# Head-wise sums of squares by four 64x64 products in the quarters of the array

## The chip, the cores and the metric

The kernel runs on one core of one Trainium2 chip. The metric is the device time of one execution in microseconds, from the first to the last instruction and what lies around them; lower is better. The matrix engine is TensorE (PE in the profile, PEld for its weight loads), the others are VectorE (DVE), ScalarE (ACT) and GpSimd (POOL); SyncE (SP) issues most DMAs. The kernel was run three times before the change, with a median of 848.72 us (846.47 to 850.33).

## The reference, cut to what matters

The program computes one layer of a hybrid model on 16 + 512 = 528 tokens of 1024 channels. One input projection of the normalised tokens feeds two groups of eight heads with 64 channels each: RWKV-7 (a recurrence over chunks) and FoX (attention with forgetting). Gates merge them, and an output projection and an MLP follow. What the change touches is a sum of squares over the 64 channels of each head, per token, in three places: RWKV's keys, FoX's queries and FoX's keys.

```python
kk = hv(k * k_k)
kk = kk / jnp.maximum(jnp.sqrt(jnp.sum(kk * kk, axis=-1, keepdims=True)), 1e-12)
...
def head_rmsnorm(t, g):
    tf = t.astype(jnp.float32)
    return tf * lax.rsqrt(jnp.mean(tf * tf, axis=-1, keepdims=True) + NORM_EPS) * g
...
q = head_rmsnorm(q.reshape(Bn, Ln, H_FX, HEAD_DIM), q_gain)
k = head_rmsnorm(k.reshape(Bn, Ln, H_FX, HEAD_DIM), k_gain)
```

## The kernel before

Channels lie on the 128 partitions and tokens along the free dimension, so a tile of 128 partitions holds two heads ("a pair"): head 0 on partitions 0 to 63, head 1 on 64 to 127. There are four pairs in each group. The stage that matters here runs from about 20 to 418 us. Its bulk are 40 blocks of the input projection: each is 128 output channels, made of 8 input blocks times three passes in the type float32r (high times high, high times low, low times high), in two parts of 264 tokens, or in one part of 512 for FoX's queries and for the 16 gate blocks. Their weights arrive as `wraw`, are split by ScalarE into `whi` and by VectorE into `wlo` (L470, L471), and the products go to the PSUM tiles `pj` (L501). Beside them run the recurrent heads (`recurrent`, `chain`, `group_norm`), the FoX features (`fox_features`: sums, normalisation, transposed values) and the attention (`attention`: scores `psc` at L611, transposed weights `ppt` at L640, mixing `py` at L656).

The order on TensorE is written out by a planner while the program is built. Each of these activities is a generator that yields the time from which it can go on, `Turns.run` picks by rank the first that is due on a model clock (`Clock`), and the projections, which have the last rank, fill the rest. In that clock a float32 matmul of the full array costs its columns divided by 600 us, one of a smaller tile columns divided by 1200, and a change of tile shape 0.1 us. TensorE keeps exactly this order; for the other engines a scheduler orders the instructions.

PSUM tiles called "sm" (`psm`, four banks) hold the small products in turn, and `banks(n)` tells when n of them come free.

A sum over the channels of a head is a matmul with `ones_blk`, the 128x128 matrix that is one where row and column belong to the same head and zero elsewhere: out of the squares (`sq`, 128 partitions) it puts each head's sum on all 64 partitions of that head. There are twelve such sums.

- RWKV's keys, one in each of four pairs (`Pair.keys`): two products of 264 columns (L754), each followed by a maximum on VectorE from PSUM into `sq` (L755); then ScalarE's logarithm and exponential (L757, L758) make the inverse root, and VectorE scales the keys `okk` (L761). From them follow `L` (L778, L781), `KT` and `BK` (L766, L767) and, on GpSimd, `BK` and `KT` again (L768 to L772), which the scores `psr` (L807) and the transposes `pbt` (L814) read.
- FoX's queries, one in each of four pairs (`normed`): one product of 512 columns (L553), ScalarE's logarithm straight from PSUM (L555), exponential (L557), and VectorE's scaling (L558).
- FoX's keys, one in each of four pairs: the same in two products of 264 columns.

The scores `psr` at L807 already use the array in quarters: `hss` are the two halves of the partitions, and each product reads one half of the rows and writes one half of the PSUM partitions, in all four combinations.

## Time and profile before

| | us |
|---|---|
| three runs: median (lowest to highest) | 848.72 (846.47 to 850.33) |
| the profiled execution: its own time | 849.18 |
| its span, first to last instruction | 847.4 |
| TensorE busy in the span | 825.8 (97%) |
| VectorE busy | 616.5 (73%) |
| ScalarE busy | 454.2 (54%) |
| GpSimd busy | 135.1 (16%) |

The granted TensorE clock was 0.999 of full speed. In the profile's rows a number such as L553 is a line of the kernel before; a tile name stands without its buffer number; "128*128" after MATMUL is the part of the array in use (rows by columns), and what follows is the shape of the result. Busy times of TensorE are made of modelled ends, so where the cost of a short group is asked, the starts of the matmuls before and behind it say more than the lengths.

### The profile page before, as it was taken

How to read it: one execution, taken by the hardware profiler on the slowest of the kernel's cores; microseconds unless marked ns; L12 is line 12 of the kernel's file. 1: busy time of each engine (PE TensorE's matmuls, PEld its weight loads, DVE VectorE, ACT ScalarE, POOL GpSimd, SP SyncE). 2: the span in 40 equal slices, each digit the busy share in tenths (PEclk: the TensorE clock that was granted, in tenths of full speed). 3: DMA queues.
4: the chain of work that ended last, by engine and by line, in shares of the span. 5: the costliest groups of instructions: out<-in, count | busy, mean ns of one | idle time of the engine just before them, and what ended most of it. 6: DMA issues, size and time to landing. Idle time of an engine off the chain costs nothing.

```text
span 847.4 us, 15278 instructions
## 1 busy us (share of the span) xinstructions
PE 825.8 (97%) x5740; PEld 678.1 (80%) x5740; DVE 616.5 (73%) x1222; ACT 454.2 (54%) x923; POOL 135.1 (16%) x133
## 2 busy tenths in 40 slices
PE   7889999999999999999999999999999999999998
PEld 6878987878887787677788779888888888888886
DVE  6996996679867965665457564876777677768688
ACT  7767536765656337644555452665355435544452
POOL 1041300004012000000022001203700560055000
PEclk9999999999999999999999999999999999999999
DMA  6231231110222212123486422651743274245421
GB/s 229 58 103 58 72 113 43 45 59 26 77 88 87 75 52 89 51 75 113 138 272 218 154 88 82 201 153 51 248 149 100 85 244 132 86 136 189 119 92 74
DMA packets 51338, 95.88 MB, mean 113 GB/s; under 512 B 5816, under 2 KB 6968, under 8 KB 51264
## 3 DMA queue, kind: packets, MB, share of 16 engines
q1 hardware_dynamic: 47680, 86.52, 32.1%
q0 software_dynamic: 1280, 4.20, 1.6%
q10 hardware_dynamic: 2304, 4.20, 1.5%
q8 instruction: 45, 0.74, 0.4%
q14 instruction: 29, 0.24, 0.1%
HBM read 88.57 MB, written 6.31 MB: 112 GB/s over the span
## 4 chain that ended last, share of the span: by engine, by line
PE 80%; DVE 5%; DMA 4%; ACT 4%; issue 2%; POOL 1%; SPq 0%; ACTq 0%; DVEq 0%; POOLq 0%
PE pj L501 25%; PE po L1150 21%; PE po L1268 12%; PE pd L1268 5%; DMA gl<-gd 2%; PE pw L858 2%; PE po L1120 2%; PE psc L611 1%; DMA wraw<-in_wo 1%; PE py L656 1%; PE ppt L640 1%; PE psr L807 1%; PE pssq L553 1%; PE pch L918 1%; PE pch L924 1%
## 5 line engine op out<-in xcount | busy, mean ns | idle before, releaser
L501 PE MATMUL pj<-uhi,whi 128*128 128x264 f32 (+1 forms) x480 | 165.7, 345 | 0.0
L501 PE MATMUL pj<-ulo,whi 128*128 128x264 f32 (+1 forms) x480 | 154.2, 321 | 1.6 <-DVE ulo L401 1.6
L501 PE MATMUL pj<-uhi,wlo 128*128 128x264 f32 (+1 forms) x480 | 154.0, 321 | 0.0
L501 PEld LDWEIGHTS pj<-uhi,whi 128*128 128x128 f32 x480 | 90.2, 188 | 15.0 <-issue 6.7
L501 PEld LDWEIGHTS pj<-ulo,whi 128*128 128x128 f32 x480 | 90.5, 188 | 8.6 <-DVE ulo L401 2.0
L501 PEld LDWEIGHTS pj<-uhi,wlo 128*128 128x128 f32 x480 | 90.3, 188 | 6.9
L236 DVE TENSOR_TENSOR wlo<-wraw,whi 128x512 fp32r<-128x512 f32 x88 | 68.2, 785 | 37.9 <-ACT whi L235 35.6
L1150 PE MATMUL po<-zhi,whi 128*128 128x512 f32 (+1 forms) x248 | 94.8, 382 | 0.0
L1150 PE MATMUL po<-zlo,whi 128*128 128x512 f32 (+1 forms) x248 | 94.8, 382 | 0.0
L1150 PE MATMUL po<-zhi,wlo 128*128 128x512 f32 (+1 forms) x248 | 94.8, 382 | 0.0
L235 ACT CAST whi<-wraw 128x512 fp32r<-128x512 f32 x88 | 53.7, 616 | 51.5 <-DMA wraw<-in_wup 19.3
L471 DVE TENSOR_TENSOR wlo<-wraw,whi 128x512 fp32r<-128x512 f32 x80 | 61.9, 781 | 17.5 <-ACT whi L470 17.0
L470 ACT CAST whi<-wraw 128x512 fp32r<-128x512 f32 x80 | 49.1, 618 | 43.8 <-PE pj L501 43.2
L270 ACT CAST whi<-t 128x512 fp32r<-128x512 f32 x64 | 39.9, 623 | 44.4 <-DVE wlo L271 20.6
L271 DVE TENSOR_TENSOR wlo<-t,whi 128x512 fp32r<-128x512 f32 x64 | 49.4, 784 | 18.8 <-ACT whi L270 18.0
L1268 PE MATMUL po<-wlo,fhi 128*128 128x512 f32 x160 | 62.7, 392 | 0.2 <-DVE wlo L271 0.2
L1268 PE MATMUL po<-whi,flo 128*128 128x512 f32 x160 | 62.3, 390 | 0.0
L1268 PE MATMUL po<-whi,fhi 128*128 128x512 f32 x160 | 62.0, 389 | 0.0
L1196 POOL TENSOR_TENSOR t<-traw 128x512 f32<-128x512 f32 x24 | 35.3, 1475 | 154.0 <-DVE wlo L271 135.8
L1150 PEld LDWEIGHTS po<-zhi,wlo 128*128 128x128 f32 x248 | 46.6, 188 | 9.0
L1150 PEld LDWEIGHTS po<-zhi,whi 128*128 128x128 f32 x248 | 46.6, 188 | 9.0
L1150 PEld LDWEIGHTS po<-zlo,whi 128*128 128x128 f32 x248 | 46.6, 188 | 9.0
(307 smaller groups left out, 1758.5 us busy)
## 6 DMA issues: line engine op xcount, KB each, us to landing
wraw<-in_win SPq DMA_DIRECT2D x84, 256.0 KB, 2.6
wraw<-in_wup SPq DMA_DIRECT2D x64, 256.0 KB, 3.4
wraw<-in_wdn SPq DMA_DIRECT2D x48, 256.0 KB, 2.6
traw<-in_wdn SPq DMA_DIRECT2D x48, 256.0 KB, 3.1
gd<-gt ACTq DMA_DIRECT2D x16, 256.0 KB, 2.3
wraw<-in_wout SPq DMA_DIRECT2D x16, 256.0 KB, 2.9
gl<-gd SPq DMA_DIRECT2D x16, 256.0 KB, 3.5
wraw<-in_wo SPq DMA_DIRECT2D x16, 256.0 KB, 3.3
```

Source lines behind the costliest of these rows:

```text
L235: A.copy(hi, raw)
L236: low.tensor_tensor(lo, raw, hi.bitcast(F32), ALU.subtract)
L270: A.copy(hi, x)
L271: V.tensor_tensor(lo, x, hi.bitcast(F32), ALU.subtract)
L470: A.copy(hi, raw)
L471: low.tensor_tensor(lo, raw, hi.bitcast(F32), ALU.subtract)
L501: mm(po, a, b[:, k, a0:a1], start=n == 0, stop=n == 23)
L858: mm(ps_[hs, n - b0, :], lhs(n)[hs], rhs(n)[hs], start=True, stop=True)
L1120: mm(po, a[:, k, 128 * i:128 * i + 128], b[:, k, :], start=n == 0, stop=n == 23)
L1150: mm(po[:, t0:t1], a, b[:, k, t0:t1], start=n == 0, stop=n == 23)
L1196: eng.tensor_tensor(t, sums[c, pair] if c in (T1, T2) else c, d, ALU.add)
L1268: mm(x[i], a[:, k, left, 128 * i:128 * i + 128], c, start=start and k == 0 and n == 0, stop=stop and k == n_pairs - 1 and n == 2)
```

## The change

Each sum is made of four products of 64 rows, 64 columns of the array and half of the tokens, in place of one or two products with the full array. The first half of the tokens goes from each half of the partitions to the same half in PSUM; the second half goes across, head 0 to partitions 64 to 127 and head 1 to 0 to 63, into a second PSUM tile. So the four products stand in the four quarters. The first PSUM tile is read by one instruction of 128 partitions as before, the second by two of 64 that put each head back in its place. Queries, which had one product and one evacuation, now have two tiles and three evacuations and ask for two free banks. The request for the activation table (`pinned`) comes behind all products.

```diff
--- before.py
+++ after.py
@@ -546,14 +546,19 @@
                 def normed(d, parts, gcol):
                     yield d["in"]
                     f, sq = d["f"], d["sq"]
-                    yield lambda: max(ck.ready(sq), banks(len(parts)))
+                    yield lambda: max(ck.ready(sq), banks(2))
                     pin = None
-                    for a0, a1 in parts:
-                        pq = psm("pssq")[:, :a1 - a0]
-                        mm(pq, ones_blk, sq[:, a0:a1], start=True, stop=True)
-                        pin = pin or pinned(d["s"])
-                        after(act(sq[:, a0:a1], pq, AF.Ln, bias=eps, scale=1.0 / 64), pin)
                     c0 = parts[0][0]
+                    half = (T - c0) // 2
+                    cuts = [slice(c0, c0 + half), slice(c0 + half, T)]
+                    pqs = [psm("pssq")[:, :half] for i in range(2)]
+                    for turn, (pq, cols) in zip((1, -1), zip(pqs, cuts)):
+                        for hs, os in zip(hss, hss[::turn]):
+                            mm(pq[os], ones_blk[hs, hs], sq[hs, cols], start=True, stop=True)
+                    pin = pinned(d["s"])
+                    for turn, (pq, cols) in zip((1, -1), zip(pqs, cuts)):
+                        for hs, os in ((slice(0, 128),) * 2,) if turn > 0 else zip(hss, hss[::-1]):
+                            after(act(sq[hs, cols], pq[os], AF.Ln, bias=eps[hs], scale=1.0 / 64), pin)
                     act(sq[:, c0:], sq[:, c0:], AF.Exp, scale=-0.5)
                     V.scalar_tensor_tensor(f, f, gcol, sq[:, c0:], ALU.mult, ALU.mult)
                     return f
@@ -749,10 +754,14 @@
                 self.sq = sq = rp.tile([128, TP], F32, name="sq")
                 s_ = act(sq[:, :T], okr, AF.Square, scale=self.col(C_KK))
                 yield lambda: max(ck.ready(sq), banks(2))
-                for hc in (slice(0, HT), slice(HT, T)):
-                    pq = psm("pkk")[:, :HT]
-                    mm(pq, ones_blk, sq[:, hc], start=True, stop=True)
-                    V.tensor_scalar(sq[:, hc], pq, 1e-24, None, ALU.max)
+                cuts = [slice(0, HT), slice(HT, T)]
+                pqs = [psm("pkk")[:, :HT] for i in range(2)]
+                for turn, (pq, hc) in zip((1, -1), zip(pqs, cuts)):
+                    for hs, os in zip(hss, hss[::turn]):
+                        mm(pq[os], ones_blk[hs, hs], sq[hs, hc], start=True, stop=True)
+                for turn, (pq, hc) in zip((1, -1), zip(pqs, cuts)):
+                    for hs, os in ((slice(0, 128),) * 2,) if turn > 0 else zip(hss, hss[::-1]):
+                        V.tensor_scalar(sq[hs, hc], pq[os], 1e-24, None, ALU.max)
                 pin = pinned(s_)
                 after(act(sq[:, :T], sq[:, :T], AF.Ln), pin)
                 act(sq[:, :T], sq[:, :T], AF.Exp, scale=-0.5)
```

The planner's clock sees other costs, so the order moves. Three places follow, before the change and with it; later lines of the changed program have higher numbers (L807 is L816, L814 is L823).

TensorE, the sum for FoX's keys of the second head pair (`pssq`), inside the chain of states (`pch`, `pyy`, transposed values `pvt`). Before:

```order
L924 MATMUL pch<-Rs,Tt 64x64 x4
L904 MATMUL pvt<-cs,ov 64x128 x2
L553 MATMUL pssq<-fsq,cs 128x264 x2
L939 MATMUL pch<-uv,bkT 64x64 x4
L947 MATMUL pyy<-uv,L_705 64x64
```

With the change:

```order
L927 MATMUL pch<-uv,L_1117 64x64
L557 MATMUL pssq<-fsq,cs 64x264 x4
L933 MATMUL pch<-Rs,Tt 64x64 x4
L913 MATMUL pvt<-cs,ov 64x128 x2
L643 MATMUL ppm<-cs,pe 16x128
```

Two products are four, and the sum has moved from behind the transposes to ahead of the state product with Tt, which uses quarters as well.

VectorE, the keys of the first head pair, from the key factor (`sg`) to KT. Before:

```order
L760 TENSOR_TENSOR sg<-sg,okk 128x528
L471 TENSOR_TENSOR wlo<-wraw,whi 128x512
L755 TENSOR_SCALAR sq<-pkk 128x264 x2
L314 MEMSET tm 128x1
L318 SCALAR_TENSOR_TENSOR orr<-pj,pr_65,tm 128x264
L471 TENSOR_TENSOR wlo<-wraw,whi 128x512
L761 SCALAR_TENSOR_TENSOR okk<-okk,pr,sq 128x528
L778 SCALAR_TENSOR_TENSOR L_705<-okk,P 128x9x63
```

With the change:

```order
L769 TENSOR_TENSOR sg<-sg,okk 128x528
L471 TENSOR_TENSOR wlo<-wraw,whi 128x512
L764 TENSOR_SCALAR sq<-pkk 128x264
L764 TENSOR_SCALAR sq<-pkk 64x264 x2
L314 MEMSET tm 128x1
L318 SCALAR_TENSOR_TENSOR orr<-pj,pr_65,tm 128x264
L471 TENSOR_TENSOR wlo<-wraw,whi 128x512
L770 SCALAR_TENSOR_TENSOR okk<-okk,pr,sq 128x528
L471 TENSOR_TENSOR wlo<-wraw,whi 128x512
L787 SCALAR_TENSOR_TENSOR L_708<-okk,P 128x9x63
```

There is one maximum more, and a conversion of weights that stood behind the second L now stands ahead of the first.

ScalarE, the logarithms for FoX's keys of the first head pair, with the evacuation of the values (`vf`). Before:

```order
L793 ACTIVATE bv<-bv,pr 128x512
L555 ACTIVATE fsq<-pssq,eps 128x264 x2
L557 ACTIVATE fsq<-fsq 128x528
L567 COPY vf<-pj 128x264
L470 CAST whi<-wraw 128x512 x2
```

With the change:

```order
L802 ACTIVATE bv<-bv,pr 128x512
L572 COPY vf<-pj 128x264
L561 ACTIVATE fsq<-pssq,eps 128x264
L561 ACTIVATE fsq<-pssq,eps 64x264 x2
L562 ACTIVATE fsq<-fsq 128x528
L470 CAST whi<-wraw 128x512 x2
```

Two logarithms are three, and a copy of the values has moved ahead of them.

## The prediction

> **What bounds the kernel now.** I read the page's first part and the chain that ended last first, then the windows by stage, then TensorE's own waits, and last the timeline around single sums. One matmul of the source in plain float32 stands in these views as two records, so the two 264-column products of one sum are "x4".
>
> ```profile
> PE 825.8 (97%) x5740; PEld 678.1 (80%) x5740; DVE 616.5 (73%) x1222; ACT 454.2 (54%) x923; POOL 135.1 (16%) x133
> PE 80%; DVE 5%; DMA 4%; ACT 4%; issue 2%; POOL 1%; SPq 0%; ACTq 0%; DVEq 0%; POOLq 0%
> ```
>
> TensorE is busy for 97% of the span and makes 80% of the chain. The sums that change lie between 46 and 319 us, inside the stretch in which projections fill every hole in TensorE's queue. Its windows (busy us and instruction count per engine, granted clock, DMA share, GB/s):
>
> ```profile
> 20.00:72.00 52.00, 46.92 (x391) 40.41 (x390) 47.62 (x90) 34.82 (x67) 9.99 (x12) 1.00 0.24 72
> 72.00:120.00 48.00, 48.00 (x381) 43.46 (x380) 39.89 (x83) 26.92 (x52) 10.23 (x10) 1.00 0.24 74
> 140.00:200.00 60.00, 58.02 (x612) 45.20 (x610) 41.91 (x137) 44.72 (x123) 3.15 (x4) 1.00 0.15 46
> 200.00:260.00 60.00, 60.00 (x507) 52.65 (x505) 46.69 (x113) 36.61 (x80) 8.86 (x10) 1.00 0.23 72
> 340.00:417.00 77.00, 76.92 (x578) 55.46 (x575) 43.78 (x141) 38.23 (x101) 0.00 (x0) 1.00 0.26 83
> ```
>
> The first column after the length is TensorE: full from 72 to 120 and from 200 to 260 us, 2 us short between 140 and 200, and full again to the end of the stage at 417. So a microsecond less of TensorE work brings the end of the stage forward by nearly one. Only the first window is different: there 5 us are idle and VectorE has 47.6 of 52 us. TensorE's waits on other engines between 40 and 345 us, ten in all, the longest and the shortest:
>
> ```profile
> PE ppt L638 <- DVE pe L627: 1.3, 1, 1.3
> PE pkk L754 <- ACT sq L750: 0.7, 1, 0.7
> PE pbt L814 <- DVE L L810: 0.4, 1, 0.4
> ```
>
> None is longer than 1.3 us and none waits for what follows a sum directly.
>
> **What the twelve sums cost now.** The groups by line and shape:
>
> ```profile
> L754 PE MATMUL pkk<-sq,cs 128*128 128x264 f32 x16 | 4.4, 399 | 0.7 <-ACT sq L750 0.7
> L553 PE MATMUL pssq<-fsq,cs 128*128 128x264 f32 x16 | 4.2, 386 | 0.0
> L553 PE MATMUL pssq<-fsq,cs 128*128 128x512 f32 x8 | 4.1, 592 | 0.0
> ```
>
> Sixteen records are eight products, thus four sums of keys (L754) and four of FoX keys (L553), 528 columns each; the last row is four sums of queries, 512 columns. Records overlap, so I take cost from starts. The timeline around one sum (start, length, engine):
>
> ```profile
> 81.50 0.28 PE L501 MATMUL pj<-uhi,wlo 128*128 128x264 f32 x1
> 81.62 1.05 PE L754 MATMUL pkk<-sq,cs 128*128 128x264 f32 x4
> 82.32 0.48 PE L501 MATMUL pj<-uhi,whi 128*128 128x264 f32 x1
> 82.64 0.28 PE L501 MATMUL pj<-ulo,whi 128*128 128x264 f32 x1
> ```
>
> From 81.50 to 82.64 are 1.14 us; two projection matmuls are in it, each 0.12 (81.50 to 81.62). The sum costs 0.90 us, or 1.70 ns a column. Eight such and four of 512 columns (0.87) make 10.7 us.
>
> **What the new form costs.** Four 64x64 products in the four quarters have a precedent, the score products of L807: twelve products of 128 columns (24 records) as four quarters, three times over. And a switch to another shape, two products of 64 rows side by side, stands at L611:
>
> ```profile
> 91.88 0.28 PE L501 MATMUL pj<-uhi,wlo 128*128 128x264 f32 x1
> 92.09 0.89 PE L807 MATMUL psr<-L,BK 64*64 64x128 f32 x24
> 92.90 0.39 PE L501 MATMUL pj<-uhi,whi 128*128 128x264 f32 x1
> 93.13 0.29 PE L501 MATMUL pj<-ulo,whi 128*128 128x264 f32 x1
> ...
> 280.14 0.39 PE L501 MATMUL pj<-uhi,wlo 128*128 128x512 f32 x1
> 280.46 0.73 PE L611 MATMUL psc<-ka,qa 64*128 64x272 f32 x4
> 281.12 0.50 PE L501 MATMUL pj<-uhi,whi 128*128 128x512 f32 x1
> 281.46 0.40 PE L501 MATMUL pj<-ulo,whi 128*128 128x512 f32 x1
> 281.69 0.39 PE L501 MATMUL pj<-uhi,wlo 128*128 128x512 f32 x1
> ```
>
> 91.88 to 93.13 is 1.25, less two projections 1.01 us. Two at a time would need six rounds of 128 columns, 1.31 us, which is more than all of it; four at a time need 0.65. So all four quarters ran at once, and 0.36 us went into leaving the full array and coming back, 0.18 for each change of shape. At L611: 1.32 less two projections of 0.23 (281.46 to 281.69) is 0.86, and 272 columns two at a time are 0.46, which leaves 0.40, or 0.20 a change. A sum by quarters between two projections is then 0.45 + 0.36 = 0.81 us against 0.90: half of the streaming is saved and nearly all of it paid back in switching.
>
> [...]
>
> Not every sum stands alone. In the order of the changed program eight of twelve lie between full-array matmuls on both sides, four touch a neighbour of another shape, and counted over TensorE's whole order the changes of shape go from 304 to 321: 17 more. So the sum on TensorE: streaming 8 x 0.45 + 4 x 0.435 = 5.3, changes 17 x 0.18 = 3.1, together 8.4 instead of 10.7: **2.3 us less**. The bounds: if changes cost nothing, 5.3 less; if the quarters ran only two at a time (at L807 two products in the same rows read the same columns, here they read different halves, which no row shows), 3.1 more, and with 24 changes of 0.20, 4.8 more. I take 2.3 less, because L807 uses the same shape and data type.
>
> **What is added behind the sums.** The second half comes out with its heads exchanged and needs two instructions of 64 partitions instead of one. The rows of the evacuations, and two copies that show that fewer partitions are not faster:
>
> ```profile
> L555 ACT ACTIVATE fsq<-pssq,eps 128x264 f32<-128x264 f32 x8 | 3.4, 475 | 0.1
> L555 ACT ACTIVATE fsq<-pssq,eps 128x512 f32<-128x512 f32 x4 | 2.8, 688 | 0.6 <-PE pssq L553 0.6
> L755 DVE TENSOR_SCALAR sq<-pkk 128x264 f32<-128x264 f32 x8 | 3.4, 431 | 2.0 <-PE pkk L754 1.9
> L906 ACT COPY uv<-pvt 64x256 f32<-64x256 f32 x36 | 13.1, 364 | 8.8 <-PE pvt L904 8.1
> L541 ACT COPY ka<-pj 128x264 f32<-128x264 f32 x8 | 3.0, 371 | 0.0
> ```
>
> ScalarE: a query sum 3 x 0.47 for 0.69 (+0.72), a FoX key sum 3 x 0.475 for 2 (+0.475), times four 4.8 us. VectorE: 4 x 0.43 = 1.7 us. Both engines have room (36.6 and 46.7 of 60 us between 200 and 260), so this is no load. It is delay: the last evacuation of a key sum ended 0.90 + 0.43 = 1.33 us after the first matmul began and now 0.18 + 0.45 + 3 x 0.43 = 1.92, +0.59; for FoX keys 0.90 + 0.475 = 1.38 becomes 2.05, +0.67; for queries 0.87 + 0.69 = 1.56 becomes 2.02, +0.46. Projections cover it, unless TensorE has none to run while it waits. That is so at one place, the first head pair:
>
> ```profile
> 49.37 0.69 DVE L471 TENSOR_TENSOR wlo<-wraw,whi 128x512 fp32r<-128x512 f32 x1 [0.91 <-ACT whi L470]
> 58.91 1.43 POOL L772 TENSOR_TENSOR KT<-BK,P 64x576 f32<-64x576 f32 x1
> 60.39 0.55 PE L814 MATMUL pbt<-cs,KT 128*128 128x128 f32 x3 [0.49 <-POOL KT L772]
> 61.94 0.87 PE L807 MATMUL psr<-L,BK 64*64 64x128 f32 x20 [0.64 <-DVE Bm L808]
> 63.18 0.52 PE L814 MATMUL pbt<-cs,KT 128*128 128x128 f32 x3 [0.38 <-DVE L L810]
> ```
>
> In the changed order VectorE has one evacuation more (0.43) and a weight conversion (0.69) ahead of the products that make KT, so the wait of the transposes on GpSimd's KT grows from 0.49 by up to 1.1 us. Queued behind them are the scores' second group and its evacuations. Against this, the conversion that moved forward is one less ahead of Bm, and the two waits on VectorE there, 0.64 and 0.38, may go: +0.1 to +1.1, I take **+0.6**. Nothing else waits for a sum: FoX's queries and keys go to scores that come several blocks later.
>
> Net: -2.3 + 0.6 = **-1.7 us**. The profiled execution took 849.18 us (span 847.4 and 1.8 around it), so 847.5. The median of the three runs shown is 0.5 lower, 848.72, which gives 847.0; I state 847.2. A measurement of this kernel tells about 0.5%, 4.2 us, from no change, so this forecast is "no change".
>
> **Rivals.**
> - *Switching hides.* If leaving and returning overlap with the full-array matmuls next to them, 5.3 - 0.6 = 4.7 us are gained: 844.0 to 844.5. Against it: 0.36 and 0.40 in two rows above. 8%.
> - *Two at a time, slower.* If two quarters that share rows cannot stream different columns at once, the streaming stays 10.7 and switching comes on top: +3.1 to +4.8, with the 0.6 852.4 to 854.1. It decides as soon as a sum takes over 0.90 us. For it: L807 never streams different columns in the same rows. Against it: each quarter's product is an instruction with a stream of its own there too. 9%.
> - *The later evacuations reach TensorE, slower.* All of the delay is 4 x 0.59 + 4 x 0.67 + 4 x 0.46 = 6.9 us; if all were waited for, 6.9 - 2.3 = +4.6, 853.3. It decides from a third on, when it eats the 2.3. The order also shifts projections around the chain of states between 140 and 200 us, where waits of 1.3 us exist already. Against it: windows full of TensorE work. 12%.
> - *The gain stops at the stage's end.* If what lies behind 417 us does not start earlier, 848.7. Against it: the first matmul there waits for evacuations that follow the last projection, and shifts with it. 10%.
>
> The forecast keeps 61%, with 845 to 850 as its own range, since a reordered program can win or lose a wait or two of 1.3 us. The range for 8 in 10 goes most of the way to the first and the second rival: **843.0 to 853.0**. Faster by over 0.5% (below 844.5): half of the first rival, a few favourable reorderings, 0.11. Slower (above 853.0): half of the second, a third of the third and a little, 0.11. Within: 0.78.
>
> **What would show it.** In the profile after: a lone sum between projections should take 0.75 to 0.85 us by starts, with its eight records begun nearly together in two groups (right), or 1.2 us and more (two at a time). Evacuations of 64 partitions should cost as much as those of 128. TensorE's wait on KT near 60 us should be 1 to 1.6 us, and the last projection should end one to three microseconds before 417.9. I am wrong if a lone sum takes 0.5 us, or if a new wait of several microseconds stands behind an evacuation.

## The result, and the profile after

The changed kernel takes **851.77 us** in the median of twenty runs (849.36 to 855.80), the kernel before 848.98 us in twenty runs beside them (846.47 to 851.02). The ratio is 1.0035, with a 95% interval of 1.0025 to 1.0045: 0.35% slower. A second group of twelve runs of the same changed program (called `changed_again` below) gave 851.33 us and 1.0015 (1.0002 to 1.0028). The change is inside the range that was forecast and within 0.5% of no change, but it went the other way: 2 to 3 us were lost where 1.7 were to be gained.

The profiled execution of the changed kernel took 855.80 us, which is the longest of its twenty. Where one nearer to the middle is needed I read `changed_again`, whose profiled execution took 852.65 us (span 850.8); it is the longest of its twelve, 1.3 us above their median. The first rows of the page of the one and the other: busy time per engine, and the shares of the chain that ended last, `changed_again` first and the slower execution behind it.

```profile
PE 825.6 (97%) x5796; PEld 675.3 (79%) x5796; DVE 617.6 (73%) x1226; ACT 457.4 (54%) x935; POOL 133.0 (16%) x133
PE 79%; DVE 6%; ACT 5%; DMA 2%; issue 2%; POOL 1%; DVEq 0%; ACTq 0%; POOLq 0%
```
```profile
PE 827.8 (97%) x5796; PEld 676.2 (79%) x5796; DVE 618.3 (72%) x1226; ACT 457.1 (54%) x935; POOL 134.7 (16%) x133
PE 75%; DVE 6%; ACT 5%; DMA 5%; issue 2%; POOL 2%; SPq 0%; DVEq 0%; ACTq 0%; POOLq 0%
```

TensorE has 56 records more (each sum now has eight), yet its busy time did not fall. The sum itself does what was forecast. The timeline of TensorE in the changed kernel, around the sum that was shown of before (start, length, engine):

```profile
81.00 0.28 PE L501 MATMUL pj<-uhi,wlo 128*128 128x264 f32 x1
81.21 0.68 PE L761 MATMUL pkk<-sq,cs 64*64 64x264 f32 x8
81.82 0.39 PE L501 MATMUL pj<-uhi,whi 128*128 128x264 f32 x1
82.05 0.28 PE L501 MATMUL pj<-ulo,whi 128*128 128x264 f32 x1
82.17 0.29 PE L501 MATMUL pj<-uhi,wlo 128*128 128x264 f32 x1
```

From 81.00 to 82.05 are 1.05 us; less two projections of 0.12 the sum costs 0.81 us, against 0.90 before. So the four quarters do run together: at the 1.70 ns a column of the sum before, their four times 264 columns two at a time would take 0.90 us, and four at a time 0.45. As an estimate from that, 0.36 of the 0.45 us that they save goes into the two changes of shape. The evacuations of 64 partitions cost what those of 128 cost: the groups of the changed kernel by line, with the shortest, median and longest in ns.

```profile
L561 ACT ACTIVATE fsq<-pssq,eps x24: 461/474/482, 76.2 to 320.0; 64x256 f32<-64x256 f32 x8, 64x264 f32<-64x264 f32 x8, 128x256 f32<-128x256 f32 x4, 128x264 f32<-128x264 f32 x4
L764 DVE TENSOR_SCALAR sq<-pkk x12: 420/430/435, 47.6 to 264.7; 64x264 f32<-64x264 f32 x8, 128x264 f32<-128x264 f32 x4
```

What is new stands in TensorE's waits between 40 and 345 us (engine, tile, line, what it waited for: us in total, times, longest). Five of the fourteen of `changed_again`:

```profile
PE pw L867 <- DVE AX L861: 2.2, 1, 2.2
PE ppt L643 <- DVE tm L314: 1.1, 1, 1.1
PE psc L616 <- DVE y_rw L995: 0.8, 1, 0.8
PE psc L616 <- DVE L L819: 0.5, 1, 0.5
PE pbt L823 <- POOL KT L781: 0.5, 1, 0.5
```

The wait on KT near 60 us is as short as before. The longest wait, 2.2 us, is that of the second group's inverse (`pw`) on VectorE's `AX`; the kernel before does not wait there at all. The windows show the place: of the kernel before and then of `changed_again` between 260 and 320 us (length, then busy us of TensorE, its weight loads, VectorE, ScalarE, GpSimd, granted clock, DMA share, GB/s).

```profile
260.00:320.00 60.00, 58.54 (x696) 48.49 (x696) 48.92 (x114) 26.32 (x62) 7.03 (x5) 1.00 0.21 67
```
```profile
260.00:320.00 60.00, 57.02 (x625) 45.98 (x624) 48.43 (x117) 26.64 (x64) 6.30 (x5) 0.97 0.22 67
```

Two things are in the second fence that I had not looked for: TensorE is 1.5 us emptier, and the granted clock is 0.97. The clock is not evenly lower: in this profile it is 0.50 from 277.8 us on for 3.41 us and full on both sides. That is 1.7 us of a full clock, as much as the whole gain that was forecast.

**The stage's sum.** For each kernel I cut the projection stage, from the first projection matmul to the last, into four parts: the streaming of all columns, TensorE's waits over 0.05 us, 1.7 us for each stretch at half clock (half of its 3.41 us), and the rest, in which the changes of shape stand. The streaming is worked out from the columns and not measured, so the rest takes up whatever that leaves; only the differences between the kernels count.

| | before | after | changed_again |
|---|---|---|---|
| stage, us | 383.6 | 385.0 | 386.3 |
| streaming | 333.5 | 328.2 | 328.2 |
| changes of shape and rest (changes) | 42.4 (296) | 46.7 (313) | 46.4 (313) |
| waits | 7.7 | 10.05 | 9.9 |
| half clock in the stage | 0 | 0 | 1.7 |
| last projection to last matmul, us | 425.1 | 429.7 | 426.1 |

The streaming falls by 5.2 us: that is half of the 6272 columns of the sums at 600 a us, the rate in the planner's clock; at the 1.70 ns a column that a sum took by starts it would be 5.3. Changes of shape and rest take 4.0 to 4.3 us of it back; what is in them follows in the section on the prediction. The waits take 2.2 us more, so that the stage is 1.0 to 1.4 us longer before any loss of clock. Behind the stage `changed_again` loses another 1.0 us. The slower execution loses 4.6 there: one stretch at half clock (1.7), waits that are 1.7 us longer, and 1.2 that I have not traced.

### The profile page after: what moved, and what is told of

It reads as the page before. It is cut to its first block, busy times and chain, and to the rows that moved or that the text cites. A ratio compares the mean times of both kernels' runs of the same rounds, so it can differ in the third digit from the quotient of the medians.

```text
span 854.0 us, 15403 instructions
## 1 busy us (share of the span) xinstructions
PE 827.8 (97%) x5796; PEld 676.2 (79%) x5796; DVE 618.3 (72%) x1226; ACT 457.1 (54%) x935; POOL 134.7 (16%) x133
## 4 chain that ended last, share of the span: by engine, by line
PE 75%; DVE 6%; ACT 5%; DMA 5%; issue 2%; POOL 2%; SPq 0%; DVEq 0%; ACTq 0%; POOLq 0%
PE pj L501 22%; PE po L1159 20%; PE po L1277 12%; PE pd L1277 5%; PE po L1129 2%; PE pw L867 2%; DMA gl<-gd 1%; DMA wraw<-in_wo 1%; PE py L661 1%; PE psc L616 1%; PE psr L816 1%; PE ppt L645 1%; POOL gl L1084 1%; PE pch L933 1%; DVE wlo L236 1%
## 5 line engine op out<-in xcount | busy, mean ns | idle before, releaser
L236 DVE TENSOR_TENSOR wlo<-wraw,whi 128x512 fp32r<-128x512 f32 x88 | 71.3, 819 | 37.5 <-ACT whi L235 37.5
L471 DVE TENSOR_TENSOR wlo<-wraw,whi 128x512 fp32r<-128x512 f32 x80 | 61.8, 782 | 12.9 <-ACT whi L470 12.6
```

The lines of the kernel that those rows point to most:

```text
L236: low.tensor_tensor(lo, raw, hi.bitcast(F32), ALU.subtract)
L471: low.tensor_tensor(lo, raw, hi.bitcast(F32), ALU.subtract)
```

## The experiments

Each kernel's ratio is to runs of the kernel before on the same chip and in the same hour. Lines of these kernels are a few numbers off those of before and after, since they carry a list. To hold the order fixed, the planner's choices were recorded from one kernel and played back in another: `Turns.run` then takes the listed stream, and a second list gives the PSUM bank of each projection block. The list by itself costs nothing that shows: the kernel before, played back from its own list (`before_warm` of experiment 5, which is changed only behind the stage), has a stage of 383.6 us, as without it.

```diff
-            at = next((i for i, t in enumerate(times) if t + self.ROOM[self.streams[i][0]] <= ck.pe + ck.SLACK), None)
+            now = turns.pop(0)
+            at = next(i for i, s in enumerate(self.streams) if s[1] == now)
```

**1. The change again: how steady is the result?** No edit.

> The changed kernel once more, for a second profile and for times on the same chip as the next three. Both theories: 851 to 853 us, about 1.0035 times before. Theory A (the planner's new order makes the loss) expects again one new wait of about 2 us near 306 us, TensorE's L867 on VectorE's L861; theory B (the quarters and their three evacuations make it) expects the loss to be spread over the twelve sums.

Measured: 851.33 us, 1.0015 (1.0002 to 1.0028). Still slower, though by less than in the first group. The waits in the stage agree with the first profile's to 0.1 us; the stretch at half clock lies elsewhere (277.8 us instead of 502.5). So the waits belong to the program and the place of the half clock does not. Both theories had expected 851 to 853 us.

**2. Is it the order or the new form?** The quarters of the change in the order of the kernel before, and the other way round, sums by the full array in the order of the changed kernel. The two edits are the change and its reverse, each with the list of the other order:

```diff
 q_in_old: the kernel before, its own order listed
-                    mm(pq, ones_blk, sq[:, hc], start=True, stop=True)
-                    V.tensor_scalar(sq[:, hc], pq, 1e-24, None, ALU.max)
+                    for hs, os in zip(hss, hss[::turn]):
+                        mm(pq[os], ones_blk[hs, hs], sq[hs, hc], start=True, stop=True)
...
 full_in_new: the changed kernel, its own order listed
-                    for hs, os in zip(hss, hss[::turn]):
-                        mm(pq[os], ones_blk[hs, hs], sq[hs, hc], start=True, stop=True)
+                    mm(pq, ones_blk, sq[:, hc], start=True, stop=True)
```

> The sums by quarters as in the change, but the planner's choices are taken from the kernel before, written out as a list, so TensorE's order is that of before except for the twelve sums themselves (changes of tile shape 319, before 304, changed 321). Theory A (the new order makes the loss): -5.2 us of streaming, 15 changes of shape at 0.18 are +2.7, up to +1 for later evacuations: ratio to before 0.997 to 0.999, 846.5 to 848.3 us. Theory B (the quarters themselves): still slower, ratio 1.002 to 1.005, 850.7 to 853.2 us.

> The sums with the full array and the evacuations as before, but with the planner's choices of the changed kernel, so TensorE runs in the changed order. Theory A: the order's loss without the quarters' gain, ratio 1.003 to 1.007, 851.5 to 855 us, with the wait near 306 us. Theory B: as before, ratio 0.999 to 1.001.

Measured: quarters in the old order 854.84 us, 1.0060 (1.0041 to 1.0079); full sums in the new order 852.51 us, 1.0036 (1.0022 to 1.0050). Neither theory stands alone. The new order by itself loses about 3 us without any quarter, and the quarters by themselves lose about 5 us in the old order, more than theory B allowed. The two do not add up: together they lost 2 to 2.8 us. In the profile of the full sums in the new order the wait of `pw` is there, and in that of the quarters in the old order the wait near 198 us has grown (the kernel before, then the quarters in its order):

```profile
PE pw L862 <- DVE AX L856: 2.2, 1, 2.2
```
```profile
PE ppt L638 <- DVE pe L627: 1.3, 1, 1.3
```
```profile
PE ppt L647 <- DVE pe L636: 1.8, 1, 1.8
```

**3. Which part of the new form?** Two kernels in the old order, each with a part of the change. `diag_in_old` puts two 64x64 products on the diagonal in place of each full one, with the evacuations as before. `split_in_old` leaves the products full, in halves of the tokens, and takes only the three evacuations.

```diff
 diag_in_old
-                    mm(pq, ones_blk, sq[:, hc], start=True, stop=True)
+                    for hs in hss:
+                        mm(pq[hs], ones_blk[hs, hs], sq[hs, hc], start=True, stop=True)
...
 split_in_old
-                    V.tensor_scalar(sq[:, hc], pq, 1e-24, None, ALU.max)
+                    for hs, os in ((slice(0, 128),) * 2,) if turn > 0 else zip(hss, hss):
+                        V.tensor_scalar(sq[hs, hc], pq[os], 1e-24, None, ALU.max)
```

> The order of before; each full-array product is replaced by two 64x64 products on the diagonal (head 0 to its own half, head 1 to its own), with the evacuations of before. Streaming stays as it was (two side by side), so this prices the changes of shape alone: 15 more than before. Theory A, with 0.18 a change: +2.7 us, ratio 1.003, a lone sum 0.90 + 0.36 = 1.26 us by starts. Theory B, in which a switch costs more than the rows showed, for instance in the weight loads behind it: over +4 us, ratio above 1.005.

> The order of before and full-array products, but each sum in two halves of the columns with the evacuations of the change: both products first, then one instruction of 128 partitions and two of 64. No change of tile shape is added (304). It prices the later evacuations alone: from the waits that stand in the trace of the quarters in the old order, +0.5 to +2 us of waits, and where one of them passes 1.6 us a half-clock stretch more; ratio 1.0005 to 1.004.

Measured: 853.07 us, 1.0043 (1.0027 to 1.0059), and 852.56 us, 1.0035 (1.0020 to 1.0051). Either part alone costs at least as much as the whole change. The first lies between its two theories. It loses on TensorE: nothing is saved in streaming, and the changes of shape and rest add up to 44.7 us (311 changes) against 42.4 (296); its stage is 1.6 us longer, and two windows at half clock behind the stage, 3.4 us, do the rest in its profile. The second has no change of shape more, and TensorE's streaming and rest are those of before within 0.5 us. Its stage is nevertheless 3.9 us longer: waits of 8.6 us against 7.7, and two stretches at half clock, 3.4 us. Without the clock's part most of the second result has no explanation; over all its executions the clock took 2.0 us of the 2.8 (the table behind experiment 7).

**4. When does the clock halve?** In the quarters in the old order it halves twice in the stage. Windows of 3.41 us that end and begin where it changes (columns as above; the granted clock is the third figure from the end):

```profile
193.36:196.77 3.41, 3.37 (x43) 2.59 (x39) 2.63 (x13) 2.45 (x8) 1.17 (x1) 1.00 0.24 79
196.77:200.18 3.41, 1.62 (x21) 1.19 (x23) 3.32 (x9) 1.73 (x5) 0.00 (x0) 1.00 0.00 0
200.18:203.59 3.41, 3.41 (x16) 2.60 (x13) 2.67 (x8) 0.89 (x2) 0.14 (x1) 0.50 0.00 0
203.59:207.00 3.41, 3.41 (x30) 3.41 (x30) 3.08 (x8) 2.85 (x7) 2.86 (x3) 1.00 0.00 0
271.86:275.27 3.41, 1.67 (x23) 0.75 (x15) 2.94 (x11) 2.06 (x7) 0.41 (x1) 1.00 0.40 129
275.27:278.68 3.41, 2.94 (x29) 2.52 (x30) 2.09 (x6) 1.40 (x4) 0.00 (x0) 0.50 0.34 107
```

In the second row TensorE is busy for 1.62 us of 3.41, with the wait of 1.8 us in it; in the next it is given half the clock for exactly one such window, and then the full clock again. The four stretches of this profile begin at 200.18, 275.27, 425.46 and 490.31 us, which are 75.09, 150.19 and 64.85 us apart, or 22, 44 and 19 windows of 3.413 us, the length that the trace of the changed kernel records for its stretch at 502.51 us: the four lie on one grid, which ran on over all the work between them. The kernel before has a wait of 1.26 us at this place and, in its profile, no such stretch before its end.

To test that as a cause, the kernel before got twelve added waits in its last stage, in `gaps_plain`: ahead of each, a small product is made to depend on a copy that VectorE makes late; its result is overwritten by the product that follows. `gaps_filled` is the same with two products of 512 columns put into each wait, whose results are overwritten too.

```diff
 gaps_plain
+                    z = dp.tile([128, 64], F32, name="z", bufs=2)
+                    V.tensor_copy(z, wait[:, 1, :64])
+                    for q in x:
+                        mm(q[:, :64], ident, z, start=True, stop=True)
...
 gaps_filled, ahead of it
+                    for _ in range(2):
+                        mm(x[_][:, :512], ident, cs[:, :512], start=True, stop=True)
```

> The kernel before with twelve added waits of TensorE in the last stage (three in each of four slices): ahead of a product stands a matmul of 64 columns, for each of its two results, on a tile that VectorE copies only after it has added up the product before; the results are overwritten. Each wait should be about 2 us. It measures by itself what a wait costs beyond its length. Theory C (over about 1.6 us of idle TensorE in one 3.41 us window is followed by 3.41 us at half clock): about 0.65 of the twelve are followed by one, 8 x 1.7 = 13 us beyond the waits' 24 us, so 880 to 892 us. Theory D (a wait costs its length): 868 to 876 us.

> The same with two matmuls on the identity (0.87 us each, overwritten) ahead of each wait, so that TensorE works through most of the same waits. Theory C: the half-clock stretches go, 10 to 14 us less than without the fillers. Theory D: the same time as without them, or a little more.

Measured: 902.76 us, 1.0616 (1.0578 to 1.0654), with the waits empty, and 888.92 us, 1.0474 (1.0450 to 1.0499), with the waits filled. Twenty-four matmuls more made it 13.8 us faster. Windows of the last stage, empty first, filled behind:

```profile
540.00:660.00 120.00, 112.35 (x488) 91.92 (x487) 82.60 (x118) 56.24 (x90) 26.42 (x20) 0.98 0.46 141
660.00:780.00 120.00, 108.87 (x448) 88.42 (x448) 72.48 (x101) 45.70 (x72) 24.50 (x17) 0.92 0.33 100
780.00:840.00 60.00, 55.42 (x234) 45.46 (x234) 37.70 (x49) 23.10 (x37) 21.05 (x15) 0.94 0.47 145
```
```profile
540.00:660.00 120.00, 119.69 (x518) 95.41 (x517) 82.78 (x119) 57.12 (x91) 25.79 (x20) 1.00 0.47 142
660.00:780.00 120.00, 115.69 (x496) 92.49 (x495) 78.89 (x108) 49.16 (x78) 30.25 (x21) 0.99 0.34 106
780.00:840.00 60.00, 57.04 (x250) 46.19 (x249) 40.59 (x57) 25.25 (x40) 16.80 (x11) 1.00 0.48 149
```

The empty kernel has eleven windows at half clock in this stage, 18.8 us lost; the filled one has one, 1.7 us. That difference, 17.1 us, is the 16.5 us between the two profiled executions (902.73 and 886.20). Over the four executions of each the clock took 17.8 us from the empty kernel and 3.6 from the filled one. So a wait on TensorE can cost more than its length (here 18.8 us of clock beside 29.4 us of waits), and the theory that it costs only its length has fallen. The empty kernel is slower than theory C had it, too (880 to 892 us): its twelve waits came to 29.4 us in the profile and not to 24, with eleven windows at half clock and not eight.

Over all seventeen profiles there are 36 windows at half clock behind 34 us. Twenty-six of them follow a window in which TensorE was idle for 1.66 us or more, and no window with so much idle time stayed without the drop. Between 1.44 and 1.63 us it fell six times and stayed at full clock ten times. Of the other four, three directly follow another window at half clock. One alone has no such explanation: the 277.8 us of `changed_again`, behind 0.81 us of idle time.

**5. Filling the waits of the kernels themselves.** Products whose results are overwritten were put into the waits: in the changed kernel two ahead of `pw`, in the quarters in the old order at four waits, in the kernel before at the starts of the output projection and of the transposes behind it.

```diff
 changed_warm
+                if g == 1 and fill:
+                    for _ in range(fill.pop()):
+                        mm(bank[:, :512], ident, cs[:, :512], start=True, stop=True)
```

> The changed kernel in its own order, with two matmuls of 128x512 added on the identity (results overwritten, 0.87 us each) at the place where TensorE waits about 2.2 us for VectorE (second head group's inverse, ahead of the first product after the block inverses). They shorten no wait, they only fill it. Theory C (a 3.41 us window with more than about 1.6 us of idle TensorE is followed by 3.41 us at half clock, 1.7 us lost): a wait of 2.17 us puts that much into one window in 70% of the window's positions, so the mean falls by about 1.2 us against the changed kernel, ratio to before 1.001 to 1.002, and no half-clock stretch stands at 305 to 309 us. Theory D (the clock has nothing to do with waits): 851.3 to 852, ratio 1.002 to 1.0035.

> The quarters in the order of before, with filling matmuls on the identity at four waits: 0.87 us ahead of the transposes that waited 1.83 us at 198 us, 0.44 and 0.65 at the two waits of 0.75 and 0.87 at 272 to 274 us, and 0.87 at the start of the output projection (1.58 us). Theory C: the half-clock stretches that the profile without fillers had at 200, 275 and 425 us go, on average 1.0 to 1.5 of them, 1.7 to 2.6 us, so 852 to 853.3, ratio 1.0035 to 1.005. Theory D: unchanged, 854 to 855.5, ratio 1.006.

> The kernel before in its own order, with one filling matmul (0.87 us) at the start of the output projection and one at the first transposes of the MLP's input, the two longest waits behind the projections (1.57 and 1.2 us in its profile). Theory C: half-clock stretches at 423 to 428 and 500 to 505 us, which profiles of other kernels here showed, become impossible: 0.3 to 1 us less than before, ratio 0.9988 to 0.9997. Theory D: 0 to 0.5 us more.

Measured: 851.86 us, 1.0027 (1.0016 to 1.0038); 853.20 us, 1.0051 (1.0034 to 1.0067); 851.01 us, 1.0012 (0.9999 to 1.0025). In the changed kernel the wait of `pw` fell from 2.17 to 0.52 us and the stage lost no clock in the profile, but the time did not fall: between 1.0015 and 1.0035 of the plain change, 1.0027 is no gain that can be told. The theory of the clock had asked for 1.2 us less, and over the twelve executions the clock took as much as without the filling, 2.0 us against 1.9. In the quarters in the old order the filling removed both stretches of the stage from the profile, and over all executions the loss of clock fell from 4.6 to 1.3 us, the level of the kernel before. The median is only 1.6 us lower, with intervals that overlap. The kernel before did not gain: it was forecast to win 0.3 to 1 us by theory C and took 1.2 us more in the mean, at the same loss of clock. So filling can bring the clock back, and the time that it saves was not shown outside the built case of experiment 4.

**6. Keys or FoX?** The quarters in the old order, once for RWKV's keys alone and once for FoX's sums alone; the edits are the two halves of the change.

> Only RWKV's four key sums by quarters with three evacuations on VectorE, FoX's eight as before, the order of before. Theory C1 (the third evacuation on VectorE lengthens the wait of the transposes on VectorE at 198 us, where the third pair's key sum stands just ahead, from 1.26 to about 1.8 us, past the 1.6): that wait is 1.7 to 1.9 us, ratio 1.002 to 1.004. Theory C2 (it comes from FoX's logarithms on ScalarE): the wait stays at 1.3, ratio 0.999 to 1.001.

> Only FoX's eight sums by quarters with three evacuations on ScalarE, the keys as before, the order of before. Streaming is 3.5 us less, twelve changes of shape at 0.22 are 2.7 more. Theory C1: the wait at 198 us stays at 1.3, ratio 0.998 to 1.001. Theory C2: the wait at 198 us is 1.7 to 1.9, ratio 1.002 to 1.005.

Measured: keys alone 852.10 us, 1.0028 (1.0018 to 1.0039); FoX alone 853.12 us, 1.0044 (1.0027 to 1.0060). The wait near 198 us, keys first, FoX behind:

```profile
PE ppt L642 <- DVE pe L631: 1.8, 1, 1.8
```
```profile
PE ppt L647 <- DVE pe L636: 1.3, 1, 1.3
```

So that wait grows by the keys, as theory C1 had it. The timeline of VectorE, in the quarters in the old order, shows how (start, length):

```profile
196.10 0.43 DVE L768 TENSOR_SCALAR sq<-pkk 128x264 f32<-128x264 f32 x1
196.45 0.15 DVE L635 RECIPROCAL rsum<-rsum 128x1 f32<-128x1 f32 x1
196.63 0.43 DVE L768 TENSOR_SCALAR sq<-pkk 64x264 f32<-64x264 f32 x1
197.08 0.59 DVE L939 COPY uv<-pch 64x128 f32<-64x128 f32 x2
197.69 0.42 DVE L768 TENSOR_SCALAR sq<-pkk 64x264 f32<-64x264 f32 x1
198.14 0.36 DVE L636 TENSOR_SCALAR pe<-pe,rsum 128x272 f32<-128x272 f32 x1
```

The third evacuation of a key sum, 0.42 us, stands just ahead of the softmax weights `pe`, for which TensorE waits. That the FoX half alone is as slow was not expected by this: its stage has 10.1 us of waits, 45.7 us of changes of shape and rest (308 changes), and one stretch at half clock. Each half has its own loss, and that of the keys is nearly all clock: 2.3 of the 2.4 us that they lose in the mean.

**7. Moving work into the wait.** Instead of adding products, turns of the projections were moved ahead of the wait, by the list alone: two turns ahead of `pw` in the changed kernel, three ahead of two waits in the kernel with keys by quarters, and the same three in the kernel before as a comparison. In the list a letter is a stream with a count ahead of it, and `e` are the projections.

```diff
 changed_moved
-c17ed8e3bc2d3e3bc
+c17ed10e3bc2de3bc
```

> The changed kernel; its planner's choices are written out and two turns of the projections (twelve matmuls of 0.12 us, no work added) are moved from behind the second group's first inverse products to ahead of them, where TensorE waits 2.17 us. Theory C: the wait falls to about 0.7 us and no half clock can follow: 1.5 + 0.7 x 1.7 = 2.7 us less than the changed kernel, ratio to before 0.999 to 1.0005. Theory D (a wait costs its length alone): 1.5 us less, 1.0008 to 1.0018. Theory E (the loss is the quarters' own and comes back in another wait): as the changed kernel, 1.002 to 1.0035.

> Only the four key sums by quarters, the order of before, and three turns of the projections moved forward without added work: two ahead of the transposes that waited 1.83 us at 199 us, one ahead of the transposes that waited 0.87 us at 275 us. The trace of the four key sums without the move has 1.9 us less of TensorE time than before in this stage and four windows at half clock. Theory C: those go, the waits fall by 1.5 to 2.2 us: ratio 0.995 to 0.998. Theory E: 1.001 to 1.003 as without the move.

> The kernel before with the same three turns moved forward: what the move is worth without quarters. Theory C: the waits of 1.26 and 0.87 us shrink by about 1.5 us together, and little half clock was there: ratio 0.998 to 0.9995. Theory E: 0.999 to 1.002.

Measured: 849.54 us, 1.0006 (0.9994 to 1.0019); 850.99 us, 1.0011 (1.0000 to 1.0022); 849.27 us, 0.9996 (0.9985 to 1.0008). The changed kernel can then not be told from the kernel before. Its timeline at the moved place, behind that of `changed_again` (the brackets hold the wait):

```profile
306.37 2.31 PE L867 MATMUL pw<-AX,Bm 64*64 64x64 f32 x72 [2.17 <-DVE AX L861]
```
```profile
305.12 2.31 PE L871 MATMUL pw<-AX,Bm 64*64 64x64 f32 x72 [1.51 <-DVE AX L865]
```

The wait fell by 0.66 us, to 1.51 and not to the 0.7 us that was expected. The edit did half of what was planned: between the last scores and `pw` TensorE now has 108 projection matmuls instead of 102, six more and not twelve, which are 0.73 us. The ratio fell by 0.001 to 0.003 against the two groups of the plain change. That is more than the 0.66 us in the middle, and the intervals do not decide it. With keys by quarters the expected gain did not come: a wait of 2.15 us on `pe` stood at 209 us instead, with a window at half clock on it; ahead of that place 42 projection matmuls are left of 54. The ratio is in theory E's range. The kernel before did not move, so the moved turns are worth nothing by themselves. No version here is measurably faster than the kernel before.

**The clock in all executions.** The mean granted clock is on record for every execution, not for the profiled ones alone. One window at half clock is 1.7 of some 850 us and takes 0.002 off it; a clock of 0.999 has none, as the profile of the kernel before shows. The lost part of the clock times the span is the loss in us; in the mean it was 1.14 us in 102 executions of the kernel before and 1.89 us in the 32 of the change, 0.75 us more. For the versions, against the executions of the kernel before in the same hour:

| version (executions) | mean time over before, us | of it more loss of clock, us |
|---|---|---|
| the change again (12) | 1.6 | 0.3 |
| quarters in the old order (6) | 5.2 | 3.2 |
| quarters in the old order, waits filled (8) | 4.0 | 0.1 |
| full sums in the new order (8) | 3.0 | 0.5 |
| products on the diagonal (12) | 3.7 | 1.8 |
| split evacuations (12) | 2.8 | 2.0 |
| keys alone (12) | 2.4 | 2.3 |
| FoX alone (5) | 3.4 | 1.8 |
| change, turns moved (11) | 0.6 | 0.6 |
| keys, turns moved (12) | 1.1 | 1.5 |

A window does not always cost its full 1.7 us. The change took 850.2 us in the mean of the 5 executions without a window, 851.3 in the 20 with one and 852.8 in the 7 with two; the kernel before 849.2 (57), 850.0 (38) and 850.2 (7). Without a window the change is 1.0 us slower than the kernel before.

## Why the prediction was right or wrong

**Right: the sum itself.** 0.45 us of streaming and 0.36 us of switching were put together to 0.81 us from the scores at L807; a lone sum took 0.81. The rival that two quarters which share rows run only one after the other has fallen, and so has the one that switching hides.

**Right: the evacuations' price.** 461 to 482 ns and 420 to 435 ns for 64 partitions, against the 475 and 431 ns that were used.

**Right: the term "changes 17 x 0.18 = 3.1", and with it "2.3 us less".** The stage's sum seems to say otherwise: 4.0 to 4.3 us for seventeen changes, 0.24 each. But the full sums in the new order and the change run the same groups in the same order and differ in the sums alone. Put side by side by the starts, the twelve sums with the group on either side of each take 2.3 us less in the change (2.4 in `changed_again`), and the quarters in the old order 2.5 less than the kernel before. Of the 5.2 us of streaming that leaves, as an estimate, 2.7 to 2.9 for the changes of shape, 0.15 to 0.18 each. What grew beyond them, 1.2 to 1.4 us, lies away from the sums, above all in groups of scores that stop half way for another engine. The largest, in the full sums in the new order and then in the change (start, length, engine; the brackets hold the wait):

```profile
236.22 1.16 PE L615 MATMUL psc<-ka,qa 64*128 64x272 f32 x8
237.31 0.39 PE L505 MATMUL pj<-uhi,whi 128*128 128x264 f32 x1
```
```profile
235.64 1.15 PE L616 MATMUL psc<-ka,qa 64*128 64x272 f32 x6
237.56 0.70 PE L616 MATMUL psc<-ka,qa 64*128 64x256 f32 x2 [0.76 <-DVE y_rw L995]
238.19 0.39 PE L501 MATMUL pj<-uhi,whi 128*128 128x264 f32 x1
```

From the first score to the next projection are 1.09 us there and 2.55 here. Only 0.76 of the 1.46 us more count as a wait. The other 0.7 us go where the last four records start one at a time, over 0.2 us apart; the unbroken group starts them in pairs. Two groups of `psr` near 96 and 98 us, which start with two of their quarters alone, lose another 0.2 and 0.4 us. Against that a group near 60 us is no longer broken and 0.5 us shorter, and what else stands in the 1.2 to 1.4 us was not traced.

**Wrong: the term "+0.6" for the waits. This is the step that failed.** I named the wait on KT near 60 us as the only place where a delay shows. There the three waits of before (0.49, 0.64 and 0.38) became one of 0.50 and one of 0.37 further on: 0.6 us shorter, not longer. The loss came from a place that the working did not look at. In the changed order TensorE's projections ahead of the second inverse are used up at 303.7 us, while VectorE's `AX` is ready only at 305.7. The two timelines of VectorE, before and in the change, with the last pair's scores, out of which the inverse is made, and the last step of `AX` (the brackets hold the wait):

```profile
277.15 0.56 DVE L808 TENSOR_TENSOR Bm<-psr,cs 128x384 f32<-128x384 f32 x1 [0.29 <-PE psr L807]
298.13 1.42 DVE L852 TENSOR_SCALAR AX<-AX,even 128x576 f32<-128x576 f32 x2
```
```profile
282.33 0.56 DVE L817 TENSOR_TENSOR Bm<-psr,cs 128x384 f32<-128x384 f32 x1 [0.16 <-PE psr L816]
304.42 1.32 DVE L861 TENSOR_SCALAR AX<-AX,even 128x576 f32<-128x576 f32 x2
```

The last scores `psr` come 5.2 us later on TensorE (281.40 instead of 276.23), and `AX` ends 6.2 us later (305.74 instead of 299.55): from the scores on, VectorE has a copy (0.78 us) and a conversion of weights (0.68 us) more to do and takes 1.0 us longer. TensorE has less to do in that time, 102 projection matmuls and six records of transposes instead of 111 and a query sum, and starts the last of them 22.0 us after the scores instead of 24.8. So it now waits 2.2 us for `AX`, where before `AX` had been ready for 1.6 us when TensorE came to it. (In `changed_again` the scores themselves come later by the stretch at half clock that begins at 277.8 us; the wait of `pw` is the same 2.2 us.) That the full sums in the new order have the same 2.2 us shows that this wait comes from the order and not from the quarters. I had read the new order at the sums and not at the waits of other work. All waits of the stage together grew by 2.2 us, and some 1.2 us went as said above, most of it in groups broken by waits, so the term is about 3.4 us and not 0.6. The last projection began at 420.0 and 420.4 us instead of 417.9, and not one to three us earlier.

**Partly right: the rival "the later evacuations reach TensorE".** It holds in the old order, where the third evacuation of the keys lengthens the wait near 198 us by 0.5 us. In the changed order that wait is 1.1 us, and the new wait of `pw` is the order's.

**Not seen: the clock.** The working took a wait at its length. Here a wait of 2.17 us holds 1.66 us or more of one 3.41 us window in two thirds of all positions of the grid ((3.41 − 2.17 + 2 x 0.51) / 3.41), so as an estimate from that share it would cost 1.1 us more on the mean. Of the three profiles with that wait one has the drop on it, the full sums in the new order at 305.4 us. Over all executions the change lost 0.75 us more of clock than the kernel before, and no less when that wait was filled, so the estimate is too high and the wait of `pw` is not shown to be what costs the clock.

**What the loss is made of.** At the sums −2.3 us, in waits +2.2 and in the broken groups and what else grew +1.2 make +1.1 us, which two profiles show; executions without a window at half clock differ by 1.0 us. The clock adds up to 0.75 us. Together that is 1.8 to 1.9 us, and the means of the 32 and the 102 executions differ by 1.9 us. That they meet so well is partly luck, since the executions come from several hours and chips, and the two groups' medians differed by 2.0 and 2.8 us from those beside them. In both profiles of the change the wait for weights at the start of the next product is also 0.9 us longer (TensorE's waits behind the stage, before and `changed_again`):

```profile
PE po L1103 <- ACT whi L235: 0.6, 1, 0.6
```
```profile
PE po L1112 <- ACT whi L235: 1.5, 1, 1.5
```

That wait ranges from under 0.3 to 1.7 us over the profiles of all kernels. Whether it costs the change anything in the mean is not settled: the 1.0 us of the executions without a window leaves little room for it.

"The gain stops at the stage's end" did not come to a test, since no gain reached it.

## What to carry to other kernels

Four products in the quarters took a small sum from 0.90 to 0.81 us here: by its columns the streaming is halved, and an estimated 0.36 us goes into leaving the full shape and coming back. So, as an estimate from that, the form pays where many such products stand together, as in the scores with twelve in 1.01 us (1.31 by columns two at a time), and little for single ones between full matmuls. Where a change moves a planner's order, look at the waits of all the work on the bounding engine in the new order, not at those of the changed instructions. In this case 1.66 us or more of idle TensorE in one 3.41 us window were followed by the half clock every time, and 1.44 to 1.63 us in six cases of sixteen: count a wait that can put so much into one window as its length and, in the executions in which the windows fall so, up to another 1.7 us; the mean granted clock of each execution shows how often. A sum that puts everything left over into one row names no cause for that row: two kernels that differ in one thing, laid side by side, showed where it lay.

## What the runs showed of the hardware

- The granted clock fell to 0.50 for one window of 3.41 us behind each of the 26 windows with at least 1.66 us of TensorE idle in seventeen profiles, and in ten other places. The grid of the windows lay elsewhere in each of three profiles: reckoned back in steps of 3.4133 us from their stretches at 502.51, 200.18 and 846.32 us, the first window starts 0.8 us into the span in the changed kernel, 2.2 in the quarters in the old order and 3.2 in the kernel before. Filling the twelve added waits with products whose results are overwritten made that kernel 13.8 us faster (902.76 to 888.92).
- Executions of the same kernel differed in length with that: the change took 850.2, 851.3 and 852.8 us in the mean with no, one and two such windows.
- Products of 64x64 in all four quarters ran together also when the two that share rows stream different columns: eight records of 264 columns started within 0.3 us (81.21 to 81.51), and the sum took 0.81 us. The same sum by two quarters on the diagonal took 1.23 us between projections:

```profile
81.68 0.28 PE L505 MATMUL pj<-uhi,wlo 128*128 128x264 f32 x1
81.89 1.11 PE L760 MATMUL pkk<-sq,cs 64*64 64x264 f32 x8
82.92 0.39 PE L505 MATMUL pj<-uhi,whi 128*128 128x264 f32 x1
83.15 0.28 PE L505 MATMUL pj<-ulo,whi 128*128 128x264 f32 x1
```
